# Four stages' operands put at other distances in SBUF by unused columns, in a decoder block on one Trainium2 core

## The chip, the core and the metric

The kernel runs on one core of one Trainium2 chip. The metric is device time in microseconds: the median over runs of the whole program. One execution is also taken by the hardware profiler; its views are quoted below.

## What is computed

The reference is one layer of a decoder block with 1024 tokens of 1024 channels, in float32:

```python
h = rms_norm(x, norm_gain) * (1.0 + scale[:, None, :]) + shift[:, None, :]
proj = h @ w_in                                   # 1024 x 8192
q, k, v, z_a, u, z_b, m_a, m_b = split(proj)      # 1024 columns each
attn = stick_breaking_attention(q, k, v)          # 16 heads of 64
p_a = (attn * silu(z_a)) @ w_branch_a
pooled = multiscale_causal_pool(u, pool_w, pool_scale)
p_b = (pooled * silu(z_b)) @ w_branch_b
merged = sigmoid(m_a) * p_a + sigmoid(m_b) * p_b
out = rms_norm(x + gate * (merged @ w_out), final_gain)
```

## The kernel before, in words

Every large product is made of three products of float32r parts: an operand is split into a high part (the value rounded to float32r) and a low part (what is left), and high x high, high x low and low x high are added up in PSUM. `split` (line 107) and `load_w` (line 122) make the two parts, `mm3` (line 159) issues the three products for each block of 128 channels. All matmuls are recorded by one helper, `order` (its inner line is 96), so the profile shows them under L96; the tile names tell the stages apart. In the profile's "out<-in", the matmul reads a moving operand (its columns stream through the array, 512 or fewer) and a stationary one (128 x 128, put there by a weight load, the PEld rows). Each matmul has its own weight load.

The stages, in order of time:

- **wm, ua, u**: the pooling maps are folded into the columns of `w_in` for u (wm: moving `phl`, stationary `wt`, 256 columns), then u is computed (moving `hT`, stationary `wg`).
- **v**, `with pool("vp")`, line 565: moving `wv` (six buffers of weights, split from `wv_raw` by ScalarE's cast at L116 and VectorE's subtraction at L111), stationary slices of `hT`. Its results leave through `vo` (L594, L595) to DRAM. Between them stand `make_lo` (low parts of later weights, `l_raw` to `wl_d`, through DMAs) and `make_d` (the pooling windows of u, read back from `u_d`).
- **wzb** and **pb**, `with pool("pb")`, line 605: z_b's projection (moving `hT`, stationary `wzb`), then the pooling branch (moving `gb`, stationary `wb`).
- **p, z, wt, av**: the projections for attention (p: moving `hT`, stationary `w`), mixed by hand with the attention's logits (z), transposes (wt, moving `ident`) and value products (av).
- **pa**, lines 921 to 960: the attention branch (moving `ga` in the pool `fing`, which is on the right side of SBUF, stationary `wa`), for one half of the tokens at a time.
- **o**, the output product, in the pool `fin`, line 928: moving `wo` (in the place of `hT`), stationary `mhl`. The last 128 tokens are cut into pieces of 512, 256 and 256 columns.

A pool is a stretch of SBUF in which its tiles lie one behind another, from the left, or from the right with `side="right"`. A tile is as wide in each of the 128 partitions as its columns need (4 bytes each). Where a tile comes to lie on bytes that earlier tiles held, the framework makes its writer wait for their last users. Nearly all tiles of the kernel are a multiple of 512 bytes wide. In the program as built, `hT` begins at byte 3552 of each partition (480 modulo 512), and so, modulo 512, do `wv`, `gb`, `ga`, `wo`, `mhl` and all weight tiles of the stages listed above except `wm` and `wt`. A block of 128 columns is 512 bytes, so the moving and the stationary operand of every matmul of v, wzb, pb, p, z, av, pa and o begin 0 bytes apart modulo 512. For wm of groups 2 and 3 the moving `phl` begins at 384 and the stationary `wt` at 480 modulo 512. The transposes have `ident` at 128 and `be` at 480.

Of the kernel before, what the change touches and what calls it, by code (L numbers as in the profile page):

```python
# [9 lines left out]
F32 = mybir.dt.float32  # L10
# [5 lines left out]
P = 128  # L16
# [38 lines left out]
def block_kernel(ctx, tc, a, out):  # L55
# [3 lines left out]
    def pool(name, **kw):  # L59
        return tc.tile_pool(name=name, bufs=1, reuse_waits="tile", **kw)  # L60
# [7 lines left out]
    def bank(tag, name):  # L68
        return psp.tile([P, 512], F32, tag=tag, bufs=BANKS[tag], name=name)
# [37 lines left out]
    def split(src, shape, pl, tag, bufs, hi_eng, lo_eng, name):  # L107
        hl = pl.tile([shape[0], 2] + list(shape[1:]), F32R, tag=tag, bufs=bufs, name=name)
        hi, lo = hl[:, 0], hl[:, 1]
        copy_to(hi_eng, hi, src)  # L110
        lo_eng.tensor_tensor(lo, src, hi.bitcast(F32), op=ALU.subtract)  # L111
        return hi, lo
# [22 lines left out]
    def make_lo(pl, n, tag=None):  # L135

        for _ in range(n):
            i = next(early_lo)
            if tag:
                raw, hi = (pl.tile([P, D], t_, tag=tag, bufs=5, name=f"l{i}_{n_}") for n_, t_ in (("raw", F32), ("hi", F32R)))  # L140
            else:
                raw = pl.tile([P, D], F32, tag="lraw", bufs=3, name=f"l{i}_raw")
                hi = pl.tile([P, D], F32R, tag="lhi", bufs=1, name=f"l{i}_hi")
            nc.sync.dma_start(raw, a["w_in"][tiles[i]])
            act.copy(hi, raw)
            v.tensor_sub(raw.bitcast(F32R), raw, hi.bitcast(F32))
            nc.sync.dma_start(wl_d[i], raw)
# [11 lines left out]
    def mm3(ps, whl, mhl, kbs, mov, first=True, last=True):  # L159
        (wh, wl), (mh, ml) = whl, mhl  # L160
        n = len(kbs)
        for i, kb in enumerate(kbs):
            for j, (w, m) in enumerate(((wh, mh), (wh, ml), (wl, mh))):
                mm(
                    ps, w[:, kb], mov(m, kb),
                    start=first and i == 0 and j == 0, stop=last and i == n - 1 and j == 2,
                )
# [4 lines left out]
    def hmov(sh):  # L172
        return lambda m, kb: m[:, kb, sh * 512:sh * 512 + 512]
# [389 lines left out]


    with pool("vp") as vp:
        def load_wv(hf, k2):
            raw = wts.tile([P, 2, 512], F32, tag="raw", bufs=2, name=f"wv{hf}_{k2}_raw")
            nc.sync.dma_start(raw.rearrange("p k c -> p (k c)"), a["w_v"][hf, k2])
            return split(raw, [P, 2, 512], vp, "wv", 6, act, v, f"wv{hf}_{k2}")

        wv = [[load_wv(0, k2) for k2 in range(4)]]
        for i in reversed(range(KB)):
            ps = bank("pj", f"u{i}_1")
            mm3(ps, whl[i], h, range(KB), hmov(1))
            use[i](1, ps)
            make_lo(vp, 1)
        early.close()
        diffs = ExitStack()
        dif = diffs.enter_context(pool("dif", side="right"))
        for hf in range(2):  # L580
            if hf == 0:
                wv.append([load_wv(1, k2) for k2 in range(4)])
            for sb in range(8):
                ss = slice(sb * P, (sb + 1) * P)
                ps = bank("pj", f"v{sb}_{hf}")
                for kb in range(KB):
                    hh, hl = h_hi[:, kb, ss], h_lo[:, kb, ss]
                    wh, wl = (w[:, kb % 2] for w in wv[hf][kb // 2])
                    for n, (l, w) in enumerate(((hh, wh), (hh, wl), (hl, wh))):
                        mm(ps, l, w, start=kb == 0 and n == 0, stop=kb == KB - 1 and n == 2)  # L590

                vo = dif.tile([P, 8, 2, HD], F32R, tag="vo", bufs=3, name=f"vo{sb}_{hf}")
                pv = ps.rearrange("p (h d) -> p h d", d=HD)
                act.copy(vo[:, :, 0], pv)  # L594
                v.tensor_sub(vo[:, :, 1], pv, vo[:, :, 0].bitcast(F32))  # L595
                nc.sync.dma_start(
                    v_d[4 * hf:4 * hf + 4, :, sb].rearrange("n p c -> p n c"),
                    vo.rearrange("p (n h) i d -> p n (h i d)", h=2).bitcast(F32),
                )
                make_lo(vp, LO_V[sb])  # L600
                if 8 * hf + sb in DIFFS:
                    make_d(DIFFS[8 * hf + sb])


    with pool("pb") as pb:
        gb = pb.tile([P, 2, KB, S], F32R, name="gb")
        for j in range(KB):
            if j not in dhls:
                make_d(j)
            zs = [pb.tile([P, 512], F32, tag="zs", bufs=3, name=f"zs{j}_{sh}") for sh in range(2)]  # L610

            def silu(sh, ps):
                z, sl = zs[sh], slice(sh * 512, sh * 512 + 512)
                act.activation(z, ps, AF.Sigmoid)
                v.tensor_mul(z, ps, z)
                v.scalar_tensor_tensor(z, dhls[j][:, sl], psc_v[:, j:j + 1], z, ALU.mult, ALU.mult)
                act.copy(gb[:, 0, j, sl], z)
                v.tensor_sub(gb[:, 1, j, sl], z, gb[:, 0, j, sl].bitcast(F32))

            project(CZB + j, f"wzb{j}", silu, act, v)  # L620
            del dhls[j]
        gacc, bg = (dif.tile([P, S + 16], F32, tag="u", bufs=2, name=n)[:, :D] for n in ("gacc", "bg"))
        nc.sync.dma_start(bg, a["b_gate"].broadcast_to([P, D]))
        for j in range(KB):
            sm = [pb.tile([P, 512], F32, tag="zs", bufs=3, name=f"sm{j}_{sh}") for sh in range(2)]
            whl = load_w(a["w_branch_b"][j], f"wb{j}", v, gp)
            wg = wts.tile([P, D], F32, tag="raw", bufs=2, name=f"wg{j}")
            nc.sync.dma_start(wg, a["w_gate"][j * P:(j + 1) * P, :])
            if j == 0:
                v.tensor_scalar_mul(gacc, wg, sc[:, 0:1])  # L630
            else:
                v.scalar_tensor_tensor(gacc, wg, sc[:, j:j + 1], gacc, ALU.mult, ALU.add)
            for sh in range(2):
                ps = bank("pj", f"pb{j}_{sh}")
                mm3(ps, whl, (gb[:, 0], gb[:, 1]), range(KB), hmov(sh))
                act.copy(sm[sh], ps)
                nc.sync.dma_start(pb_d[j][:, sh * 512:sh * 512 + 512], sm[sh])
            make_lo(dif, LO_PB[j], "d")

        ones_r = pb.tile([P, P], F32R, name="ones_r")  # L640
        act.copy(ones_r, ones)
        ghl = split(gacc, [P, D], pb, "ghl", 1, act, v, "ghl")
        for hf in range(2):
            sl = slice(hf * 512, hf * 512 + 512)
            ps = bank("z", f"gate{hf}")
            for i in range(2):
                mm(ps, ones_r, ghl[i][:, sl], start=i == 0, stop=i == 1)
            v.tensor_add(bg[:, sl], ps, bg[:, sl])
        nc.sync.dma_start(g_d, bg[0:1, :])
# [5 lines left out]
    with pool("at") as at:  # L655
# [88 lines left out]
        def load_ga(sh, ps):  # L744
            ga = []
            for p in ps:
                r_ = fing.tile([P, 512], F32, tag="gr", bufs=3, name=f"gr{sh}_{p}")
                ins = (act if sh == 0 else nc.sync).dma_start(r_, ga_d[p][:, sh * 512:sh * 512 + 512])
                if sh == 1:
                    tc.keep_in_program_order(ins)  # L750
                g_ = fing.tile([P, 2, 512], F32R, tag="ga", bufs=12, name=f"ga{sh}_{p}")
                act.copy(g_[:, 0], r_)
                v.tensor_sub(g_[:, 1], r_, g_[:, 0].bitcast(F32))
                ga.append(g_)
            return ga
# [156 lines left out]
        for p in range(NP):  # L912
            used = 0
            for k in range(8):
                upto = QUANTA[p] * sum(SHARE[:k + 1]) // sum(SHARE)
                step(ahead.get(p * 8 + k, []), p * 8 + k, upto - used)
                used = upto
                if p * 8 + k == max(ahead):

                    logits.close()  # L920
                    fing = ctx.enter_context(pool("fing", side="right"))
                    ga = load_ga(0, range(NP - 1))
        pinned[0] = False
        ga += load_ga(0, [NP - 1])
        fill(10000)


    with pool("fin") as fin:

        def load_wo(kb):  # L930
            wr = fin.tile([P, D], F32, tag="wor", bufs=2, name=f"wor{kb}")
# [134 lines left out]
```

## Time and profile before

| what | us |
|---|---|
| median of 3 runs | 1216.24 (1215.61 to 1216.5) |
| profiled execution | 1219.15 |
| its span, first to last instruction | 1217.4 |
| TensorE matmuls busy | 1204.6 (99%) |
| TensorE weight loads busy | 1000.7 (82%) |
| VectorE / ScalarE / GpSimd busy | 793.7 / 558.0 / 202.4 |

The profiled execution is 2.9 us above the median of the runs. Busy time of matmuls overlaps itself, since one begins before the last has drained: the pace of a run of matmuls is read from the starts in the timeline, by dividing the time between two starts by the number of matmuls between them. A timeline row gives the start, the time to the end of the last instruction in it, the engine, the line, the operation, the tiles, the shape of the first one and, behind x, how many instructions follow each other in it.

### The profile page before, as it was taken

The numbers are of one execution on the slowest core, as the hardware profiler recorded it, in microseconds if no ns is written. First come the engines' busy times: TensorE is split into PE (matmuls) and PEld (weight loads), VectorE is DVE, ScalarE is ACT, GpSimd is POOL, SyncE is SP. The second block draws the span as 40 slices with busy tenths as digits, with TensorE's granted clock in tenths as the row PEclk, the third lists the DMA queues.
The fourth block names the chain that finished last, engine by engine and source line by source line (L and its number), as shares of the span: only waits on it lengthen the run. The fifth ranks groups of instructions, "written<-read, shape, count | busy, mean of one in ns | idle before, by whom it ended". The sixth has DMA issues, their size and how long they took to land.

```text
span 1217.4 us, 16017 instructions
## 1 busy us (share of the span) xinstructions
PE 1204.6 (99%) x5750; PEld 1000.7 (82%) x5750; DVE 793.7 (65%) x1075; ACT 558.0 (46%) x1041; POOL 202.4 (17%) x361
## 2 busy tenths in 40 slices
PE   8999999999999999999999999999999999999997
PEld 7888878888888888888888888888888888888886
DVE  6754475567511388777868778787786763785643
ACT  5564233234302365665656656665655653232211
POOL 1000000000222343222213223221312210000001
PEclk9999999999999999999999999999999999999999
DMA  9649999226943311322424124242233235985622
GB/s 359 258 163 319 322 357 347 70 87 223 317 143 115 136 52 61 102 79 98 130 96 130 62 91 126 96 131 82 83 104 105 95 112 171 346 283 177 217 64 84
DMA packets 73090, 194.53 MB, mean 160 GB/s; under 512 B 7730, under 2 KB 21170, under 8 KB 70836
## 3 DMA queue, kind: packets, MB, share of 16 engines
q1 hardware_dynamic: 62244, 174.44, 41.9%
q10 hardware_dynamic: 10768, 19.08, 4.8%
q8 instruction: 45, 0.74, 0.2%
q14 instruction: 33, 0.27, 0.1%
HBM read 138.96 MB, written 50.34 MB: 155 GB/s over the span
## 4 chain that ended last, share of the span: by engine, by line
PE 89%; DMA 4%; DVE 4%; issue 2%; ACT 2%; POOL 0%; POOLq 0%; ACTq 0%; DVEq 0%; SPq 0%
PE p L96 34%; PE pb L96 7%; PE wzb L96 7%; PE pa L96 7%; PE o L96 6%; PE z L96 5%; PE v L96 5%; PE av L96 5%; PE wt L96 5%; PE ua L96 3%; PE wm L96 2%; DMA l_raw<-in_w_in 2%; PE u L96 2%; DMA wl_d<-l_raw 1%; DVE be L96 1%
## 5 line engine op out<-in xcount | busy, mean ns | idle before, releaser
L96 PE MATMUL p<-hT,w 128*128 128x512 f32 x1920 | 534.3, 399 | 0.2 <-DVE kl L96 0.2
L96 PEld LDWEIGHTS p<-hT,w 128*128 128x128 f32 x1920 | 341.4, 188 | 56.2 <-DVE kl L96 0.6
L793 DVE TENSOR_TENSOR_SCAN om<-om 128x512 f32<-128x512 f32 (+7 forms) x128 | 175.8, 1373 | 49.1 <-ACT om L786 25.7
L786 ACT ACTIVATE om<-z 128x512 f32<-128x512 f32 (+2 forms) x192 | 94.5, 492 | 104.9 <-PE z L96 78.1
L813 DVE TENSOR_TENSOR wt<-wt,wt 128x512 fp32r<-128x512 f32 (+1 forms) x160 | 100.8, 630 | 60.6 <-ACT wt L812 59.2
L791 POOL TENSOR_SCALAR_AFFINE_SELECT om<-om 128x128 f32<-128x128 f32 x128 | 68.1, 532 | 333.6 <-ACT om L786 309.6
L812 ACT CAST wt<-wt 128x512 fp32r<-128x512 f32 (+1 forms) x160 | 87.2, 546 | 65.3 <-PE wt L96 63.5
L96 DVE TENSOR_TENSOR be<-be,om 128x511 f32<-128x511 f32 (+7 forms) x128 | 101.3, 799 | 1.0 <-DVE om L793 0.5
L96 PE MATMUL av<-wt,vv 128*128 128x512 f32 x320 | 94.2, 375 | 0.0
L787 ACT ACTIVATE be<-z 128x512 f32<-128x512 f32 (+2 forms) x192 | 93.6, 488 | 0.0
L96 PEld LDWEIGHTS wt<-ident,be 128*128 128x128 f32 x576 | 72.3, 140 | 24.2 <-DVE wt L813 2.6
L96 PE MATMUL wt<-ident,be 128*128 128x128 f32 x576 | 89.0, 272 | 1.6 <-DVE wt L813 1.6
L96 PE MATMUL pa<-ga,wa 128*128 128x512 f32 x384 | 89.6, 389 | 0.1
L96 PE MATMUL v<-wv,hT 128*128 128x512 f32 x384 | 88.1, 390 | 1.6 <-DVE vo L595 1.6
L96 PE MATMUL o<-wo,mhl 128*128 128x512 f32 (+1 forms) x408 | 89.6, 377 | 0.0
L96 PE MATMUL wzb<-hT,wzb 128*128 128x512 f32 x384 | 87.2, 389 | 0.0
L96 PE MATMUL pb<-gb,wb 128*128 128x512 f32 x384 | 87.2, 389 | 0.0
L96 PEld LDWEIGHTS v<-wv,hT 128*128 128x128 f32 x384 | 71.8, 188 | 17.7 <-DVE vo L595 2.8
L96 PEld LDWEIGHTS o<-wo,mhl 128*128 128x128 f32 x408 | 73.5, 188 | 14.1
L96 PEld LDWEIGHTS pa<-ga,wa 128*128 128x128 f32 x384 | 72.0, 188 | 15.4 <-DVE wa L111 0.5
L96 PEld LDWEIGHTS wzb<-hT,wzb 128*128 128x128 f32 x384 | 72.1, 188 | 15.0
L96 PEld LDWEIGHTS pb<-gb,wb 128*128 128x128 f32 x384 | 72.1, 188 | 15.0
(134 smaller groups left out, 1421.4 us busy)
## 6 DMA issues: line engine op xcount, KB each, us to landing
w_raw<-in_w_in SPq DMA_DIRECT2D x40, 512.0 KB, 4.4
l_raw<-in_w_in SPq DMA_DIRECT2D x32, 512.0 KB, 6.2
wl_d<-l_raw SPq DMA_DIRECT2D x32, 512.0 KB, 5.3
w<-wl_d SPq DMA_DIRECT2D x32, 512.0 KB, 3.8
v_d<-vo SPq DMA_DIRECT2D x16, 512.0 KB, 5.5
vv<-v_d SPq DMA_DIRECT2D x8, 1024.0 KB, 5.8
wa_raw<-in_w_branch_a SPq DMA_DIRECT2D x16, 512.0 KB, 4.8
wa<-in_w_mod SPq DMA_DIRECT2D x7, 1024.0 KB, 6.4
```

Of the source, the lines that this page charges most:

```text
L96: ins = op(*args, **kw)
L786: act.activation(om[:, b0:b0 + n], zp[:, :n], AF.Sigmoid, scale=-0.125)
L787: act.activation(be[:, b0:b0 + n], zp[:, :n], AF.Sigmoid, scale=0.125)
L791: gp.affine_select(out=tl[:, :P], in_=tl[:, :P], pattern=[[1, P]], compare_op=ALU.is_gt, fill=fill, base=0, channel_multiplier=-1)
L793: v.tensor_tensor_scan(om[:, :W], om[:, :W], om[:, :W], 1.0, ALU.mult, ALU.min)
L812: act.copy(wt[:, 0, :off], pt[:, :off])
L813: v.tensor_sub(wt[:, 1, :off], pt[:, :off], wt[:, 0, :off].bitcast(F32))
```

## The change

Four tiles that nothing reads or writes are put into pools: 64 columns (256 bytes) into `vp`, 96 (384 bytes) into `pb`, 8 (32 bytes) into `fing` and 48 (192 bytes) into `fin`. In three of them the tile comes first, and the tiles behind it move up by its width; `fing` ends at the right edge, and its `ga` tiles move down by 32 bytes.

```diff
     with pool("vp") as vp:
+
+        vp.tile([P, 64], F32, name="skip_v")
         def load_wv(hf, k2):
...
     with pool("pb") as pb:
+        pb.tile([P, 96], F32, name="skip_pb")
         gb = pb.tile([P, 2, KB, S], F32R, name="gb")
...
                     fing = ctx.enter_context(pool("fing", side="right"))
                     ga = load_ga(0, range(NP - 1))
+                    fing.tile([P, 8], F32, name="skip_pa")
...
     with pool("fin") as fin:
+        fin.tile([P, 48], F32, name="skip_o")
 
         def load_wo(kb):
```

In the program as built, the operands of the four stages then begin at these distances from each other (moving minus stationary, modulo 512 bytes):

| stage | moving, stationary | matmuls | distance before | after |
|---|---|---|---|---|
| v | `wv`, `hT` | 384 | 0 | 256 |
| pb | `gb`, `wb` | 384 | 0 | 384 |
| pa | `ga`, `wa` | 384 | 0 | 480 |
| o | `wo`, `mhl` | 408 | 0 | 320 |

All other products keep their distances. Other tiles of the four pools (`zs`, `bg`, `fg`, `s_`, `m_`, `b_`, `y` and more) move along by the same number of bytes. Each engine has the same instructions in the same order as before. Six of them wait for other things than before, since tiles that moved lie on other old bytes. On ScalarE, where the casts of the first two weights of v stand (wv) behind the last rows of h, this was:

```order
L536 ACTIVATE hT<-hf_7_808,mods 128x512 [waits DVE_49]
L116 CAST wv_0_835<-wv_0_raw 128x1024
L116 CAST wv_1_840<-wv_1_raw 128x1024
L145 CAST l_hi<-l_raw 128x1024 [waits DMAHW3_49,DVE_49]
L192 COPY u_sg_878<-u_1_853 128x512 [waits DMAHW1_49,PE_49]
```

and in the changed program, at the same place:

```order
L536 ACTIVATE hT<-hf_7_808,mods 128x512 [waits DVE_49]
L116 CAST wv_0_836<-wv_0_raw 128x1024 [waits DVE_49]
L116 CAST wv_1_841<-wv_1_raw 128x1024
L145 CAST l_hi<-l_raw 128x1024 [waits DMAHW3_49]
L192 COPY u_sg_879<-u_1_854 128x512 [waits DMAHW1_49,PE_49]
```

The wait for VectorE (its last low part of h) has gone from the third cast to the first. Of the other four, the load of the first `l_raw` on SyncE's queue gains a wait for VectorE, the third one's loses a wait for GpSimd; VectorE's subtraction for the first `wv` gains a wait for an earlier load; one such wait moves from its fourth to its fifth; and ScalarE's cast of the third `ga` loses a wait for GpSimd.

## Rows read from the trace of the kernel before

**Rows 1.** Busy time, share of the span and instructions of each engine (the page).

```profile
PE 1204.6 (99%) x5750; PEld 1000.7 (82%) x5750; DVE 793.7 (65%) x1075; ACT 558.0 (46%) x1041; POOL 202.4 (17%) x361
```

**Rows 2.** The chain that ended last, its shares by engine (the page).

```profile
PE 89%; DMA 4%; DVE 4%; issue 2%; ACT 2%; POOL 0%; POOLq 0%; ACTq 0%; DVEq 0%; SPq 0%
```

**Rows 3.** Matmul groups (the page): line, engine, operation, out<-in, shape, count | busy, mean.

```profile
L96 PE MATMUL v<-wv,hT 128*128 128x512 f32 x384 | 88.1, 390 | 1.6 <-DVE vo L595 1.6
L96 PE MATMUL o<-wo,mhl 128*128 128x512 f32 (+1 forms) x408 | 89.6, 377 | 0.0
```

**Rows 4.** Stretches of TensorE: us, busy (count), granted clock; this is pb.

```profile
core 0: us, PE busy (x), PEclk, DMA share, GB/s
...
304.94:391.98 87.04, 87.04 (x385) 1.00 0.57 197
```

**Rows 5.** Timeline of TensorE, 210 to 410 us.

```profile
218.15 87.20 PE L96 MATMUL wzb<-hT,wzb 128*128 128x512 f32 x384
305.19 87.20 PE L96 MATMUL pb<-gb,wb 128*128 128x512 f32 x384
392.23 1.07 PE L96 MATMUL gate<-ghl,ones_r 128*128 128x512 f32 x4
```

**Rows 6.** Timeline of TensorE, end of o, from two of its 256-column pieces on.

```profile
1205.33 5.80 PE L96 MATMUL o<-wo,mhl 128*128 128x256 f32 x47
...
1210.61 0.52 PE L96 MATMUL o<-wo,mhl 128*128 128x256 f32 x3
```

**Rows 7.** Timeline of TensorE, fp32 products of the start.

```profile
15.93 7.07 PE L96 MATMUL wm<-praw,wt 128*128 128x256 f32 x32
22.84 1.04 PE L96 MATMUL xt<-ident,x 128*128 128x128 f32 x8
```

**Rows 8.** Timeline of TensorE, 489 to 500 us, within attention.

```profile
492.03 1.52 PE L96 MATMUL p<-hT,w 128*128 128x512 f32 x6
493.39 0.50 PE L96 MATMUL av<-wt,vv 128*128 128x512 f32 x2
...
494.77 1.55 PE L96 MATMUL p<-hT,w 128*128 128x512 f32 x6
496.16 0.60 PE L96 MATMUL wt<-ident,be 128*128 128x128 f32 x4
...
497.76 0.86 PE L96 MATMUL p<-hT,w 128*128 128x512 f32 x3
498.46 0.51 PE L96 MATMUL av<-wt,vv 128*128 128x512 f32 x2
```

**Rows 9.** Timeline of TensorE, 66 to 79 us, wm products of group 3.

```profile
66.95 3.02 PE L96 MATMUL wm<-phl,wt 128*128 128x256 f32 x24
69.81 1.07 PE L96 MATMUL u<-hT,wg 128*128 128x512 f32 x4
```

**Rows 10.** Timelines of ScalarE and VectorE, 66 to 100 us.

```profile
89.12 1.99 ACT L116 CAST wv<-wv_raw 128x1024 fp32r<-128x1024 f32 x2
...
95.19 0.59 ACT L192 COPY u_sg<-u 128x512 f32<-128x512 f32 x1 [3.13 <-PE u L96]
...
67.14 0.29 DVE L96 TENSOR_SCALAR diag<-ident,st 128x128 f32<-128x128 f32 x1 [0.99 <-POOL st L246]
...
89.24 0.75 DVE L537 SCALAR_TENSOR_TENSOR hT<-hf,mods,hT 128x512 fp32r<-128x512 f32 x1 [0.79 <-ACT hT L536]
```

**Rows 11.** Timeline of SyncE's queue, 60 to 92 us.

```profile
69.06 21.76 SPq L144 DMA_DIRECT2D l_raw<-in_w_in  x3
```

**Rows 12.** Timeline of TensorE, the first part of v.

```profile
128.64 16.48 PE L96 MATMUL v<-wv,hT 128*128 128x512 f32 x72
145.44 11.19 PE L96 MATMUL v<-wv,hT 128*128 128x512 f32 x48 [0.31 <-DVE vo L595]
157.93 60.38 PE L96 MATMUL v<-wv,hT 128*128 128x512 f32 x264 [1.30 <-DVE vo L595]
```

**Rows 13.** Chain that ended last, one of its longest pieces: start us, us, what.

```profile
149.03 6.91 DMA u<-u_d
```

## The prediction, written before the changed kernel ran

> **What bounds the kernel now.** I read the busy shares first, then the chain that ended last, then the timeline of the stages that the change touches. TensorE is busy for 99% of the span and holds 89% of the chain [rows 1, 2], so what one matmul costs is paid in full almost everywhere. The touched stages are products of float32r operands with 512 moving columns: 384 each for v [rows 3], pb and pa (by the table of the change), and 408 for o, of which the cut of the last 128 rows into pieces of 512, 256 and 256 makes 2 x 24 = 48 of 256 columns and leaves 360 of 512. [...]
>
> The reader should take one number from the stage that is cleanest: pb starts at 305.19, its successor at 392.23, and 384 matmuls lie between [rows 5]. That is 87.04 / 384 = 226.7 ns each. The wzb stage before it gives the same, (305.19 - 218.15) / 384 = 226.7. [...]
>
> **Is 226.7 the floor, and does distance matter at all?** Two stretches of this trace speak of that. In all the stages above the moving and the stationary operand are 0 bytes apart modulo 512.
>
> First, the same p matmuls, at distance 0, run off that pace after the order of shapes was disturbed. In the stretch of 489 to 500 us, six of them take (496.16 - 494.77) / 6 = 231.7 ns, three take (498.46 - 497.76) / 3 = 233.3, while six others take (493.39 - 492.03) / 6 = 226.7 [rows 8]. So 226.7 is a settled state that this pairing of addresses falls into, not the cost of each possible one: off it, this shape costs 5.0 ns more.
>
> Second, one stretch has another distance. The wm products of group 3 read rows that lie 96 bytes below their weights modulo 512. 24 of them, of 256 columns, take (69.81 - 66.95) / 24 = 119.2 ns [rows 9], against the 120.0 of o at distance 0. They do not settle on 120.0. So I take distance to matter, but at 256 columns leaving the settled state costs nothing; it gains 0.8.
>
> **The change part by part.** (1) The four unused tiles issue no instruction: their cost is 0. (2) They shift later tiles, so six instructions change what they wait for. The one that could matter: ScalarE's first cast of wv now waits for VectorE's last low half of h, and starts when that ends, 89.24 + 0.75 = 89.99, instead of at 89.12. ScalarE idles 3.13 us just behind these casts, and v's first matmul starts at 128.64, so 0.9 us vanishes [rows 10, 12]. The other five lie beside it or lose a wait; no queue gains one that ends later than what it already waited for: SP's load of l_raw waits in addition for a VectorE scaling that is over by 67.43 (67.14 + 0.29), while it is issued at 69.06 [rows 10, 11]. (3) The new distance, moving minus stationary modulo 512, is 256 in v, 384 (minus 128) in pb, 480 (minus 32) in pa and 320 (minus 192) in o. The p, wzb, u, z, av and transpose products keep theirs. What one matmul at these distances costs, no row of before shows. Its bounds: the row of the same shape off the settled state gives +5.0 ns, the row of another distance but half the columns gives -0.8. The first is nearer, since 512 columns are what the four stages stream; I weigh it two to one: (2 x 5.0 - 0.8) / 3 = +3.1 ns.
>
> How many pay: pb 384, pa 384, o 360. Of v only those behind its second stop count: it stands idle 0.31 us before its 73rd matmul and 1.30 us before its 121st [rows 12], and the chain ahead of that runs through a 6.91 us DMA of u from u_d that VectorE needs, not through TensorE [rows 13]. The first 72 + 48 = 120 matmuls, 120 x 3.1 = 0.4 us, fit into that idle time; without that cover they would cost those 0.4 us. The remaining 264 pay. Sum: (384 + 384 + 360 + 264) x 3.1 = 1392 x 3.1 = 4.3 us; the 48 short ones of o at -0.8 give back 0.04. **Forecast: +4.3 us, slower by 0.35%.** The profiled execution, 1219.15 us with a span of 1217.4, would go to 1223.5; it stands 2.9 above the median of the runs, 1216.24, so the median goes to **1220.5 us**. Next late behind these stages: nothing, they hand over to other TensorE work.
>
> **The rivals.** *No effect.* [...] Then 1216.2 us. For it: wzb and pb agree to 0.1 ns [rows 5] although their moving operands lie in different tiles, 64 KB long. Against it: wm at another distance. [...]
>
> [...]
>
> *Worse than the forecast.* All 1392 at 233.3, the dearest of the rows: 1392 x 6.6 = 9.2 us, 1225.4 us.
>
> *The change does not do what it says* (the tiles get no place): no effect again, 1216.2; the built program puts them in, so it has no chance of its own.
>
> **How the numbers follow.** A measurement of this kernel tells about 0.2% (2.4 us) from no change. Slower by more has 0.47: the forecast (0.38) and the worse case (0.09). Within 0.2% has 0.29: the rival of no effect, and surpluses of under 1.7 ns. Faster by more has 0.24: one stage freed 0.17, more than one 0.07. The bounds of the unknown price give 1216.24 - 1392 x 0.8 = 1215.1 and 1216.24 + 1392 x 5.0 = 1223.2. The range reaches down to one stage freed and up to near the worse case, **1211.8 to 1225.0**, which leaves out about 0.07 and 0.08. The forecast's own range, as cases of both signs have weight, is 1218.7 to 1223.2.
>
> **What would show it.** In the profile after: the mean of pb, 87.04 us for 384 matmuls before, at 88.2 (229.8 ns); v behind its last stop, pa and o likewise; wzb, p and u as before. If pb, v, pa and o keep 226.7, distance means nothing at this shape. [...] If the stages differ, the distance of each tells which part of it counts. I am wrong in mechanism if the time moves while these four paces stand still.

## The result and the profile after

The changed kernel takes 1222.38 us (median of 5 runs, 1221.35 to 1223.01) against 1216.39 for the kernel before (5 runs): 6.0 us more, a ratio of 1.0044 with a 95% interval of 1.0033 to 1.0055. The forecast was 1220.5 us, slower, in a range of 1211.8 to 1225.0.

The groups of the page that answer to [rows 3] (busy us, mean ns of one matmul, idle before):

```profile
L96 PE MATMUL pa<-ga,wa 128*128 128x512 f32 x384 | 92.0, 396 | 0.0
...
L96 PE MATMUL o<-wo,mhl 128*128 128x512 f32 (+1 forms) x408 | 90.1, 378 | 0.0
L96 PE MATMUL pb<-gb,wb 128*128 128x512 f32 x384 | 89.8, 395 | 0.0
L96 PE MATMUL v<-wv,hT 128*128 128x512 f32 x384 | 87.2, 389 | 0.0
```

pb is busy for 89.8 us instead of 87.2, a single matmul of it for 395 ns; v's 389 ns are those of wzb in both kernels. The pace shows it better. The timeline of TensorE in the changed kernel, from v to the gate, and from pa to the end (start, time to the end of the last, shape, count):

```profile
128.79 87.20 PE L96 MATMUL v<-wv,hT 128*128 128x512 f32 x384
215.83 87.20 PE L96 MATMUL wzb<-hT,wzb 128*128 128x512 f32 x384
302.87 89.75 PE L96 MATMUL pb<-gb,wb 128*128 128x512 f32 x384
392.46 1.09 PE L96 MATMUL gate<-ghl,ones_r 128*128 128x512 f32 x4
393.39 21.95 PE L96 MATMUL p<-hT,w 128*128 128x512 f32 x96
...
1036.54 22.56 PE L96 MATMUL pa<-ga,wa 128*128 128x512 f32 x96
1058.94 5.66 PE L96 MATMUL o<-wo,mhl 128*128 128x512 f32 x24
...
1111.68 22.14 PE L96 MATMUL o<-wo,mhl 128*128 128x512 f32 x96
1133.66 8.81 PE L96 MATMUL pa<-ga,wa 128*128 128x512 f32 x36
...
1144.39 11.35 PE L96 MATMUL pa<-ga,wa 128*128 128x512 f32 x48
1155.58 1.54 PE L96 MATMUL o<-wo,mhl 128*128 128x512 f32 x6
```

The same view near its end, from the first of the 256-column pieces of o, and from the fourth last:

```profile
1208.74 5.60 PE L96 MATMUL o<-wo,mhl 128*128 128x256 f32 x48
...
1213.73 0.62 PE L96 MATMUL o<-wo,mhl 128*128 128x256 f32 x4
```

The same stretches of p, pa and o in the kernel before:

```profile
393.13 21.92 PE L96 MATMUL p<-hT,w 128*128 128x512 f32 x96
...
1036.22 21.92 PE L96 MATMUL pa<-ga,wa 128*128 128x512 f32 x96
1057.98 5.60 PE L96 MATMUL o<-wo,mhl 128*128 128x512 f32 x24
...
1109.66 21.92 PE L96 MATMUL o<-wo,mhl 128*128 128x512 f32 x96
1131.42 8.68 PE L96 MATMUL pa<-ga,wa 128*128 128x512 f32 x36
```

Divide the time between two starts by the matmuls between them, stage by stage:

| stage | distance now | ns per matmul before | after | matmuls | us |
|---|---|---|---|---|---|
| v | 256 | 226.7 away from its stops | (215.83 - 128.79) / 384 = 226.7 | 384 | 0 |
| wzb | 0 | 226.7 | (302.87 - 215.83) / 384 = 226.7 | 384 | 0 |
| pb | 384 | 226.7 [rows 5] | (392.46 - 302.87) / 384 = 233.3 | 384 | +2.55 |
| pa | 480 | (1057.98 - 1036.22) / 96 = 226.7 | 233.3 for the first 96, 233.1 for a later 48 | 384 | +2.5 |
| o, 512 columns | 320 | (1131.42 - 1109.66) / 96 = 226.7 | (1133.66 - 1111.68) / 96 = 229.0 | 360 | +0.8 |
| o, 256 columns | 320 | (1210.61 - 1205.33) / 44 = 120.0 [rows 6] | (1213.73 - 1208.74) / 44 = 113.4 | 48 | -0.3 |

That is 5.5 us, of the 6.0 measured, well within the interval (4.0 to 6.7 us). From the start of p to the start of pa nothing moved: 1036.54 - 393.39 = 643.15 us, against 1036.22 - 393.13 = 643.09 before.

The spans of the two profiled executions differ by less, 1220.6 - 1217.4 = 3.2 us. In the execution of before, v stood still for its results' way out, twice by [rows 12], and a few matmuls behind each stop were slower (the 264 from the second on took (218.15 - 157.93) / 264 = 228.1 ns each); its stage took 218.15 - 128.64 = 89.51 us, and 87.04 in the execution after. Without these 2.5 us of one execution the spans differ by 5.7. Such stops of v come and go between the executions of the kernels below as well, whatever their distances (none in five of them, 0.16 to 0.28 us in three), so I don't count them to the change. The execution after has a stop that before has not, 0.85 us in u for ScalarE's `wg`; v begins at 128.79 against 128.64 all the same, so the 5.7 us hold nearly nothing of it.

### The profile page after: what moved, and what is told of

The parts are those of the page before. It is cut to its first block, busy times and chain, and to the rows that moved or that the text cites. A ratio compares the mean times of both kernels' runs of the same rounds, so it can differ in the third digit from the quotient of the medians.

```text
span 1220.6 us, 16015 instructions
## 1 busy us (share of the span) xinstructions
PE 1208.7 (99%) x5750; PEld 1000.3 (82%) x5750; DVE 794.1 (65%) x1075; ACT 557.8 (46%) x1041; POOL 201.6 (17%) x361
## 4 chain that ended last, share of the span: by engine, by line
PE 93%; DVE 3%; ACT 2%; issue 1%; DMA 1%; POOL 0%; POOLq 0%; ACTq 0%; DVEq 0%
PE p L96 34%; PE pa L96 7%; PE pb L96 7%; PE wzb L96 7%; PE v L96 7%; PE o L96 6%; PE z L96 5%; PE av L96 5%; PE wt L96 5%; PE u L96 4%; PE ua L96 3%; PE wm L96 1%; DVE be L96 1%; DVE om L796 1%; DVE kl L96 1%
## 5 line engine op out<-in xcount | busy, mean ns | idle before, releaser
L96 PE MATMUL pb<-gb,wb 128*128 128x512 f32 x384 | 89.8, 395 | 0.0
L96 PE MATMUL v<-wv,hT 128*128 128x512 f32 x384 | 87.2, 389 | 0.0
L96 PE MATMUL wzb<-hT,wzb 128*128 128x512 f32 x384 | 87.2, 389 | 0.0
```

The costliest lines, as they stand in the source:

```text
L96: ins = op(*args, **kw)
```

## The experiments

Four theories were to be told apart: **distance** (what a matmul costs is set by how far apart its moving and its stationary operand begin), against **place** (it is set by where one operand lies), **stage** (each stage has its own price off its old place) and **waits** (part of the 6 us comes from the waits that moved with the tiles; in the programs as built there are eight such instructions, not six). To move the weights of wzb, p, pa and o at once, an unused tile goes to the front of the weight pool, and what lies behind that pool (`wv`, `gb`, and the `be` of the transposes) moves along; the 1024 bytes for it are taken from a scratch area ahead of all tiles, which moves everything by a multiple of 512. The expectations name the distances, and the programs as built have them. Each engine keeps its instructions, their order and, in e1 to e4, e6 and e7, all its waits.

### e1: everything moved, distances kept

```diff
     wts = ctx.enter_context(pool("wts"))
+    edge = ctx.enter_context(pool("edge", side="right"))
+    edge.tile([P, 96], F32, name="skip_r")
...
+    const.tile([P, 32], F32, name="skip_c")
     ident = const.tile([P, P], F32, name="ident")
...
-    nc = bacc.Bacc(..., dynamic_dma_scratch_size=2048)
+    nc = bacc.Bacc(..., dynamic_dma_scratch_size=1024)
```

> Every tile is moved up by 128 bytes modulo 512 (96 instead of 480), so each pair of operands keeps distance 0; no wait changes. If the distance sets the pace: v, wzb, pb, pa and o stay at 226.7 ns for 512 columns, the short pieces of o at 120.0, and the time stays at 1216.4 us within 0.2%. If the place of one operand by itself sets it: paces leave 226.7 in all these stages together, towards the 229 to 233 ns of the changed kernel, and 1560 matmuls at 2 to 7 ns give 1220 to 1227 us.

Measured: 1216.18 us against 1216.42, ratio 0.9998 (0.9989 to 1.0008). The timeline of TensorE in e1:

```profile
127.49 87.20 PE L99 MATMUL v<-wv,hT 128*128 128x512 f32 x384
214.53 87.20 PE L99 MATMUL wzb<-hT,wzb 128*128 128x512 f32 x384
301.57 87.20 PE L99 MATMUL pb<-gb,wb 128*128 128x512 f32 x384
388.61 1.07 PE L99 MATMUL gate<-ghl,ones_r 128*128 128x512 f32 x4
```

All three at 87.04 / 384 = 226.7 ns, and pa and o as well. Moving all operands by 128 bytes changes nothing in these stages as long as they stay equally far from each other: **place** falls, as far as one shift can tell. The smaller scratch area, which the next kernels have too, costs nothing either.

### e2, e3, e4: the weight pool moved by 128, 192 and 64 bytes

```diff
     wts = ctx.enter_context(pool("wts"))
+    wts.tile([P, 32], F32, name="skip_w")      # e3: 48, e4: 16
...
     with pool("pb") as pb:
+        pb.tile([P, 64], F32, name="skip_pb")  # e3: 32, e4: 16
...
-    nc = bacc.Bacc(..., dynamic_dma_scratch_size=2048)
+    nc = bacc.Bacc(..., dynamic_dma_scratch_size=1024)
```

> Weight pool moved by 128 bytes, gb by 256 more. Distances: v 128, wzb, p, pa and o 384, pb 256. If the pace is a function of the distance alone with a period of 256 bytes: pb at 226.7 ns, and v, wzb, pa and o at the 233.3 that pb had at 384 in the changed kernel, o's short pieces unknown. If it has a period of 512, v at 128 may differ from the 233.3, while wzb, pa and o at 384 must show it. If the stage matters and not the distance: pb stays at 233.3, v and o at 226.7 and 228.9.

> Weight pool moved by 192 bytes, gb by 128 more. Distances: v 192, wzb, p, pa and o 320, pb 128. Distance alone: wzb, pa and o at the 228.9 ns that o had at 320 in the changed kernel, o's short pieces at 113.3, pb at 233.3 (128, as at 384). p, which at distance 0 is settled for a part only (mean 230.4 without the restarts), would come to about 229 throughout: 1.5 ns less for some 1600 matmuls, 2.4 us, against 2.2 ns more for 384 of wzb, 384 of pa and 360 of o (2.5 us) and 6.7 more for 384 of pb (2.6 us): 1219 us. Stage and not distance: wzb and p as before, pa at 233.2, pb at 233.3: 1222 us.

> Weight pool moved by 64 bytes, gb by 64 more. Distances: v 64, wzb, p, pa and o 448, pb 64. New distances, but 64 is 320 modulo 256: with a period of 256 bytes v and pb come to 228.9 ns; with one of 512 they may come to anything. 448 (192 modulo 256) has not been seen; if the sign does not matter it is like 64, 228.9. If only multiples of 256 settle, all of these stages lie above 226.7 and the time above 1219 us, unless p gains.

One run each: e2 1230.55 us, e3 1225.77, e4 1230.63. The timelines of TensorE, of e2 first:

```profile
128.32 89.75 PE L97 MATMUL v<-wv,hT 128*128 128x512 f32 x384
217.91 89.76 PE L97 MATMUL wzb<-hT,wzb 128*128 128x512 f32 x384
307.51 87.22 PE L97 MATMUL pb<-gb,wb 128*128 128x512 f32 x384
394.57 1.07 PE L97 MATMUL gate<-ghl,ones_r 128*128 128x512 f32 x4
395.47 22.55 PE L97 MATMUL p<-hT,w 128*128 128x512 f32 x96
...
1043.46 22.46 PE L97 MATMUL pa<-ga,wa 128*128 128x512 f32 x96
```

Read pb first: at 256 it is back at (394.57 - 307.51) / 384 = 226.7 ns, while v, which was settled at 256 in the changed kernel, now pays (217.91 - 128.32) / 384 = 233.3 at 128, and wzb, which no earlier kernel had moved, 233.3 at 384. The same stages, with prices exchanged as their distances are: **stage** falls, and **distance** stands. pa and o at 384 came out a little below the 233.3 that was expected, at 232.3 and 232.4. The stretch from p to pa, with p at 384, grew from 643.1 to 647.99 us.

e3:

```profile
218.02 88.07 PE L97 MATMUL wzb<-hT,wzb 128*128 128x512 f32 x384
305.93 89.39 PE L97 MATMUL pb<-gb,wb 128*128 128x512 f32 x384
395.16 1.08 PE L97 MATMUL gate<-ghl,ones_r 128*128 128x512 f32 x4
396.07 22.16 PE L97 MATMUL p<-hT,w 128*128 128x512 f32 x96
...
1041.31 22.14 PE L97 MATMUL pa<-ga,wa 128*128 128x512 f32 x96
```

wzb at 320 takes 87.91 / 384 = 228.9 ns, what o took there. pb at 128 takes 89.23 / 384 = 232.4, close to the 233.3 of v at the same distance in e2, but not the same. Two expectations missed. p at 320 was to gain 2.4 us within attention, since it is settled there for a part only; from p to pa it took 1041.31 - 396.07 = 645.24 us, 2.1 more than before. Added up from each start to the next, p took 0.9 us more there, and z and av, whose own distance stayed 0, 0.5 and 0.7 more: what stands between the moved matmuls pays too. With that, and with v at 192 (233.9 behind a stop), the time came out 7 us above the 1219 that I had set down. And o's short pieces were to take 113.3 ns at 320, as in the changed kernel; they took 117.8.

e4:

```profile
127.58 88.08 PE L97 MATMUL v<-wv,hT 128*128 128x512 f32 x384
215.50 89.75 PE L97 MATMUL wzb<-hT,wzb 128*128 128x512 f32 x384
305.09 88.06 PE L97 MATMUL pb<-gb,wb 128*128 128x512 f32 x384
392.99 1.07 PE L97 MATMUL gate<-ghl,ones_r 128*128 128x512 f32 x4
393.90 22.56 PE L97 MATMUL p<-hT,w 128*128 128x512 f32 x96
...
1043.18 22.56 PE L97 MATMUL pa<-ga,wa 128*128 128x512 f32 x96
```

v and pb at 64 take 229.0 and 228.9 ns, as wzb and o do at 320: a period of 256 bytes fits. wzb at 448 takes 89.59 / 384 = 233.3, so the sign counts: 64 below is dearer than 64 above. p at 448 made its stretch 649.28 us long, 6.2 more.

### e5: only the tiles of v and o

```diff
     with pool("pb") as pb:
-        pb.tile([P, 96], F32, name="skip_pb")
...
-                    fing.tile([P, 8], F32, name="skip_pa")
```

(the edit against the changed kernel)

> Only two of the four unused tiles: v at distance 256, o at 320; pb and pa back at 0. If the paces of the changed kernel are all there is: v 226.7 ns (no cost, with the moved waits of its tiles), o 360 x 2.2 - 48 x 6.7 = +0.5 us, pb and pa at 226.7, so 1216.9 us: of the 6.0 us, 5.0 hung on pb and pa. If the moved tiles' waits or a cost of v take a share, the time stays above 1218.5 us.

Measured: 1216.91 us against 1216.43, ratio 1.0004 (0.9995 to 1.0013). The timeline of TensorE in e5, pb and two places among o's 256-column pieces:

```profile
302.53 87.20 PE L96 MATMUL pb<-gb,wb 128*128 128x512 f32 x384
389.57 1.07 PE L96 MATMUL gate<-ghl,ones_r 128*128 128x512 f32 x4
...
1203.54 5.82 PE L96 MATMUL o<-wo,mhl 128*128 128x256 f32 x48
...
1208.72 0.63 PE L96 MATMUL o<-wo,mhl 128*128 128x256 f32 x4
```

pb is back at 226.7 ns. The short pieces, at the same distance 320 as in the changed kernel, took (1208.72 - 1203.54) / 44 = 117.7 ns this time, so o makes 360 x 2.3 - 48 x 2.3 = 0.7 us; 0.5 was measured. The operands of o lie on the same bytes in both programs, so this difference of 4 ns comes from neither distance nor place; its cause is open. Seven of the eight moved waits are in this kernel, all that gained a wait among them (the eighth, the cast of the third `ga`, only loses one): **waits** get no share that can be measured. 5 of the 6 us hang on pb and pa, as their paces say.

### e6, e7: 32 and 96 bytes; e8: inside the 32 bytes

e6 and e7 are e2 with 8 and 24 columns in both places. e8 leaves the pools alone and begins `gb` and `mhl` a few columns into wider tiles:

```diff
+        off = {"wv": 0, "mhl": 2}.get(tag, 0)
+        if off:
...
+            hl = pl.tile([shape[0], 2 * w + 128], F32R, tag=tag, bufs=bufs, name=name)[:, off:off + 2 * w]
...
-        gb = pb.tile([P, 2, KB, S], F32R, name="gb")
+        gb = pb.tile([P, 2 * KB * S + 8], F32R, name="gb")[:, 4:4 + 2 * KB * S]
+        gb = gb.rearrange("p (i k s) -> p i k s", i=2, k=KB)
```

> Weight pool moved by 32 bytes, gb by 32 more. Distances: v 32, pb 32, wzb, p, pa and o 480. With a period of 256 bytes 480 gives about 233.2 ns as pa had it in the changed kernel, in wzb and o too, and p rises by 2 ns or more, so over 1228 us. 32 has not been seen: if two reads that begin near each other hurt whichever is ahead, v and pb come to about 233 as well; if the sign counts (64 gave 228.9, 448 gave 233.3), they lie below, at 227 to 230.

> Weight pool moved by 96 bytes, gb by 96 more. Distances: v 96, pb 96, wzb, p, pa and o 416. Not seen yet. Between 64 (228.9) and 128 (232.4 to 233.3), so v and pb at 229 to 233 ns; 416 lies between 384 and 448, which both gave 232 to 233, so wzb, pa and o at 232 to 234 and the time at 1230 us. [...]

> Distances finer than the 32 bytes of the allocator: gb begins 16 bytes into its tile (pb 16), mhl 8 bytes into its tiles (o 504); the rest as before. If what counts is the step of 32 bytes or more, pb and o stay settled at 226.7 ns. If each 16 bytes counts, pb leaves 226.7 and o, whose stationary rows then begin within a group of 16 bytes, may leave it too. If distance 0 is special only because both reads begin alike, both come to 229 to 233.

One run each: e6 1233.81 us, e7 1234.54, e8 1220.00. Timelines of TensorE, e6:

```profile
127.87 89.77 PE L97 MATMUL v<-wv,hT 128*128 128x512 f32 x384
217.47 89.76 PE L97 MATMUL wzb<-hT,wzb 128*128 128x512 f32 x384
307.06 89.76 PE L97 MATMUL pb<-gb,wb 128*128 128x512 f32 x384
396.66 1.08 PE L97 MATMUL gate<-ghl,ones_r 128*128 128x512 f32 x4
```

e7:

```profile
217.66 90.12 PE L97 MATMUL wzb<-hT,wzb 128*128 128x512 f32 x384
307.62 89.77 PE L97 MATMUL pb<-gb,wb 128*128 128x512 f32 x384
397.23 1.09 PE L97 MATMUL gate<-ghl,ones_r 128*128 128x512 f32 x4
...
1220.76 5.74 PE L97 MATMUL o<-wo,mhl 128*128 128x256 f32 x47
...
1225.98 0.52 PE L97 MATMUL o<-wo,mhl 128*128 128x256 f32 x3
```

e8:

```profile
302.69 89.11 PE L96 MATMUL pb<-gb,wb 128*128 128x512 f32 x384
391.64 1.08 PE L96 MATMUL gate<-ghl,ones_r 128*128 128x512 f32 x4
...
1109.56 22.31 PE L96 MATMUL o<-wo,mhl 128*128 128x512 f32 x96
1131.71 8.69 PE L96 MATMUL pa<-ga,wa 128*128 128x512 f32 x36
```

32 costs as much as 480 (v, wzb and pb all 233.3), 96 gives 89.61 / 384 = 233.4 and 416 gives 89.96 / 384 = 234.3, the dearest. e7 missed its expected 1230 us by 4.5: pb and v (at least 233.4 ns) lie above the 229 to 233 set down for them, and the stretch from p to pa, with p at 416, was 4.9 us longer than before. Its short pieces of o, at the same 416, took (1225.98 - 1220.76) / 44 = 118.6 ns, less than at 0. In e8, pb at 16 leaves the settled pace (88.95 / 384 = 231.6), and so does o at 504, 8 bytes below its weights: (1131.71 - 1109.56) / 96 = 230.7. So neither of the two, both less than 32 bytes off distance 0, is free.

All together, for 512 columns:

| distance modulo 256 | stages that had it (distance modulo 512) | ns |
|---|---|---|
| 0 | all of before, e1; v (256); pb (256) | 226.7 |
| 16 | pb (16) | 231.6 |
| 32 | v, pb (32) | 233.3 |
| 64 | v, pb (64); o, wzb, pa (320) | 228.9 to 229.0 |
| 96 | pb (96) | 233.4 |
| 128 | v, pb (128); pb, wzb, pa, o (384) | 232.3 to 233.3 |
| 160 | wzb, pa, o (416) | 234.3 |
| 192 | wzb, pa, o (448) | 233.3 |
| 224 | pa, wzb, o (480) | 233.1 to 233.3 |
| 248 | o (504) | 230.7 |

v at 96 and at 192 is left out, since it stood still in between; behind its stop, with the restart in it, it took 233.8 and 233.9. The period of 256 bytes rests on three pairs: 0 and 256, 64 and 320, 128 and 384. e2 to e4 and e6 to e8 ran once each, so a number here is the pace of 96 or 384 matmuls in one execution. No distance that ran is below 226.7, so none of them beats the kernel before: only the 48 short pieces of o gained, 0.3 us, less than a measurement tells.

## Why the prediction was right, and where its sizes were off

- **What bounds the kernel.** TensorE's pace was paid in full: 5.5 us in the paces, 6.0 in the time. Of the four paces that were to move, three did (pb, pa, o), and wzb and p stood still as forecast.
- **"226.7 is a settled state, not the cost of each possible pairing."** Right: every distance that is no multiple of 256 left it, always upwards. That its price could be read from rows at distance 0 was luck. The off-state rows [rows 8] gave 231.7 and 233.3 ns, and the distances of pb and pa gave 233.3 and 233.1, but no run shows that the two have one cause. At 512 columns the pace fell below 226.7 at no distance that ran.
- **"Distance matters", from the wm rows [rows 9].** Right, shown by e1, e2 and e4. The row was even a fair guide for its own shape: at its distance, 416, o's 256-column pieces took 118.6 ns in e7, 1.4 below the 120.0 of distance 0. But it was no guide to 512 columns, where the same 416 is the dearest (wzb in e7, 234.3) and the distances off the multiples of 256 cost 2.2 to 7.6 ns, nor to the changed kernel's short pieces, which at 320 gained 6.6 ns rather than 0.8 (2.3 in e5).
- **One price for all four stages, 3.1 ns, from weighing 5.0 against -0.8.** This is the term that was mis-sized. v pays 0, o 2.3, pb and pa 6.7 and 6.5. The forecast of 4.3 us was the sum of a stage charged for nothing (v, 0.8 us) and two charged at half their price (pb and pa, 1.2 each for 2.5); the upper bound of 5.0 ns was too low for them, and the 6.6 ns of the worse rival was their price. No row supported the weights of two to one, and the errors of v, and of pb and pa, partly cancelled: that the sum came within 1.7 us of the measured 6.0 is partly luck.
- **v's cover.** It was not needed: v costs nothing at 256, and the two stops under which its first 120 matmuls were to hide are not in the execution after.
- **The moved waits at nothing.** Right: ScalarE's first cast of `wv` now waits for VectorE, 0.82 us in the execution after, and v begins when it did. e5 holds seven of the eight and shows 0.5 us, no more than o's pace makes.
- **The rivals.** "No effect" falls with pb and pa. At 384 pb takes 233.3 ns, at 0 and at 256 it takes 226.7, with the same instructions. "One stage freed", to which the range reaches down and which has 0.17 of the chances, is a term that no run shows: 4.4 us (1216.24 - 1211.8) from one stage of 384 matmuls would be 11.6 ns each, and at 512 columns none of the nine other distances modulo 256 came below 226.7. Only the short pieces of o went that way, from 120.0 to 113.4 ns (117.7 in e5).

What stays open: why the distance counts at all, and why the period is 256 bytes. The table shows what each distance costs; the runs don't show why.

## What to carry to other kernels

Where TensorE streams float32r blocks of 512 columns back to back, each with its own weight load, keep moving and stationary operands a multiple of 256 bytes apart: 0 and 256 gave 226.7 ns here, and of the distances tried, all others cost 1.0 to 3.4% per matmul, and two unused tiles of 32 bytes, one of them in front of a weight pool, cost this kernel 1.4% (e6, one run, 1233.81 against 1216.43). Tiles whose widths are all multiples of 256 bytes do it by themselves if they begin alike; a small constant tile, or a margin of a few columns, between two pools undoes it without one instruction changed. To see it, divide the time between two stage starts by the matmuls between them: the means of single matmuls moved by 6 to 7 ns in 390, the pace by 3%.

## What the runs showed that I had not expected

- The best distance depends on the number of columns: at 512 columns 0 is the cheapest of all that ran (226.7) and 64 the next (228.9); at 256 columns 320 is cheaper than 0, 113.4 ns (117.7 in e5, 117.8 in e3) against 120.0.
- The sign counts: 64 bytes above the weights costs 228.9, 64 below 233.3.
- The same distance modulo 256 need not give one number: 128 gave 232.4 in pb of e3 and 233.3 in v of e2, 320 gave o's short pieces 113.4 and 117.7, on the same bytes. Distances 0 and 256 gave 226.7 in every stage that ran undisturbed.
- 8 bytes are enough to leave the settled pace (o in e8, 230.7 ns).
- The float32 transposes of attention (128 columns) were moved too, from 160 bytes (modulo 512) to 32, 480, 96, 128 and 64 in e2, e3, e4, e6 and e7. In the changed kernel, where they kept 160, one takes 272 ns, as before; no figure here tells what one takes at the other distances, so what is shown holds for the float32r products.
